# Chains first in the even mixer, and the odd mixer's running sums by transfers, its heads in pairs

## The chip, the cores and the metric

One of the eight cores of a Trainium2 chip runs the whole kernel. A core has TensorE (PE, with its weight loads shown apart as PEld), VectorE (DVE), ScalarE (ACT), GpSimd (POOL) and SyncE (SP), whose instruction streams run beside each other and meet at semaphores, and 16 DMA engines. The metric is the device time of one launch in microseconds. The kernel before takes 3082.39 us, the median of three runs (3081.61 to 3086.01).

## The reference

A decoder trunk of two layers over 288 tokens: 256 of a prompt and 8 x 4 new tokens of samples with 2048 tokens of past. Layer 0 mixes tokens by a gated MLP and a sparse attention (the "even mixer"), layer 1 by a Mamba-2 state space scan (the "odd mixer"); a gated MLP with a short convolution follows each.

```python
hp = hp + mp; hs = hs + ms                            # mixer of rmsnorm(h)
hp = hp + fp; hs = hs + fs                            # conv_ffn of rmsnorm(h)

# even mixer, samples: compressed attention, ranking, selected blocks
o_c, p_c = cmp_attend(q, k_cmp, v_cmp, pos)           # 2 x 64 blocks of cached pages
idx = select_blocks(p_c, pos, nb)                     # top 16 blocks of 64 tokens
o_s = sel_attend(q_rot, pos, idx, kb, vb)

# odd mixer: 64 heads in 8 groups, chunks of 128
acs = jnp.cumsum(dt * a, axis=-1)                     # running sums of each head
mix = cb[:, :, None] * jnp.exp(segsum(dt * a))        # exp(acs_i - acs_j), j <= i
y_diag = jnp.einsum('bgecij,bcjgep->bcigep', mix, xdt)
y_off = jnp.einsum(...) * jnp.exp(acs)
```

All is fp32. Products with weights are made from high and low parts: x_hi w_hi + x_lo w_hi + x_hi w_lo.

## The kernel before, in words

**The weight stream.** All weights pass once, as 6880 tiles of 128x128 ("slots"), each with three matmuls of 288 columns on PE ("mains": `xh,whi`, `xl,whi`, `xh,wlo`, or `hidh`/`hidl`), 20640 in all. A load `wraw<-in_w` on SP's queue brings 8 slots (512 KB, five buffers). Of each four slots ScalarE casts the high part (`whi`) and VectorE makes the low one (`wlo`). Results are summed in a PSUM tile `acc`, of which there are `PMAIN` = 2 beside five tiles `ps` for everything else. An evacuation multiplies by the reciprocal root mean square of the token (`rstd`) and writes it as `h`; it can run only once `make_rstd` (832) has made `rstd`: sums, a square root, a transposition `hl`, a spread over partitions by the matmul `ps<-rb,ones_r`, a copy.

**Phases.** The even mixer lasts from 0 to about 525 us, its MLP to 1370, the odd mixer to 2243, the second MLP to 3079.

**The order of the work.** It is planned when the program is built. Everything beside the stream is a generator, a "job"; `Trunk.step` (561) takes its next instruction and, when the planner's clock says that the inputs are ready and the engine free (within 0.02 us), writes it into the engine's stream, else it lets the job sleep. `tick` (600) steps the jobs in the order of their list between the mains. So each engine's order is fixed in the program, and an instruction whose input comes late holds up all behind it on its engine. `want` takes a buffer of a pool and `rel` gives it back.

**Even mixer.** `weigh` (1964) and `pool_blocks` (1990) read pages of the cache by gathers (`st<-in_ccmp,ptc`) and weigh them; `sample_cmp` (2032) attends to the compressed blocks, `rank` (2084) counts for each block how many beat it, and `sample` (2006) gathers the 16 chosen blocks and attends to them (`ps<-st,qzr` for scores, `po<-st,PT` for values).

**Odd mixer.** `dt_chain` (1093) makes the steps and, by matmuls with triangles, the running sums. They stay in SBUF as `csh`: 64 rows of high parts and 64 of low parts, a row for each head. The eight groups of heads come one after another: `ssd_old` (1290) reads and writes the samples' states (`po<-h,cms`, `xdd`), `ssd_new` (1304) adds to them (`ps<-xst,bst`), and `ssd_heads(g, q)` (1324) makes two heads: for each, a matmul with a column of `selc` spreads its running sums over 128 partitions (`ps<-csh,selc`), ScalarE makes L = relu(cs - csum), its exponentials, and `ec`; POOL multiplies `ec` with C; VectorE makes `mx` and, for the samples, `mxs`. Ten matmuls for each pair, a "burst" with weights 64 columns wide, then sum the outputs: `ps<-mx,xdt`, `ec,st`, `cmat,xdd`, `mxs,xds`.

In the profile all instructions carry the line of the helper that records them, L391 (L390 in the changed kernel), so they are told apart by tiles.

Of the kernel before, what the change touches and what calls it, by code (L numbers as in the profile page):

```python
# [10 lines left out]
F32 = mybir.dt.float32  # L11
F32R = mybir.dt.float32r
# [113 lines left out]
for _n, _w in (("tle", 128), ("tgt", 128), ("ble", 32), ("bgt", 32), ("selc", 64), ("srep", 32), ("srepT", 128),  # L126
               ("tmask", 256)):
    MATS[_n] = (sum(w for _, w in MATS.values()), _w)
# [387 lines left out]
class Job:  # L516
    def __init__(self, gen, at, room):
        self.gen, self.at, self.room, self.item, self.held = gen, at, room, None, []

class Trunk:
    def __init__(self, tc, I, O):
        self.clk = Clock()
        self.tc, self.I, self.O = tc, I, O
        self.nc, self.off = (Engines(tc.nc, self.clk, off) for off in (False, True))
        self.jobs, self.bg = [], []
        self.nbg, self.at, self.puts = 3, 0.0, 0
# [32 lines left out]
    def step(self, j):  # L561

        sent = None
        while True:
            self.cur = j
            if j.item is None:
                try:
                    j.item = j.gen.send(sent)
                except StopIteration:
                    for n in j.held:  # L570
                        Slots.back(n)
                    return False
# [24 lines left out]
            sent = it.pool.give(*it.a)  # L597
            j.held.append(sent.tensor.name)

    def tick(self):  # L600
        self.jobs = [j for j in self.jobs if j.at > self.now or self.step(j)]
        for j in list(self.bg)[:self.nbg]:
            if j.at <= self.now and not self.step(j):
                self.bg.remove(j)

    def wait(self, cond):

        for _ in range(200000):
            if cond():
                return  # L610
            self.at = max(self.now, min(j.at for j in self.jobs + self.bg[:self.nbg]))
            self.tick()
        raise RuntimeError([(j.gen.__name__, j.item) for j in self.jobs + self.bg])
# [46 lines left out]
    def run(self):  # L660
        tc, nc = self.tc, self.nc
        with ExitStack() as st:
            pool = lambda n, b, **k: Slots(st.enter_context(tc.tile_pool(name=n, bufs=b, **k)), b, self.clk)
            self.cst = pool("cst", 1)
            self.wraw = pool("wraw", 5)
            self.wsp = pool("wsp", AHEAD + 1)
            self.xp = pool("xp", 1)
            self.rms = pool("rms", 4)
            self.hsp = pool("hsp", 1, space=bass.MemoryType.DRAM).tile([128, KD, T], F32, name="hsp")
            self.pmain = pool("pmain", PMAIN, space=bass.MemoryType.PSUM)  # L670
            self.pold = pool("pold", 1, space=bass.MemoryType.PSUM)
            self.pside = pool("pside", 7 - PMAIN, space=bass.MemoryType.PSUM)
            st.enter_context(tc.manual_schedule())
            self.body()

    def body(self):
# [86 lines left out]
        self.wait(lambda: not self.jobs)  # L763
# [22 lines left out]
    def leave(self):  # L786
        if self.pst is not None:
            self.wait(lambda: not self.jobs)
            self.pst.close()
            self.pst = None  # L790
# [144 lines left out]
    def enter_f(self, l):  # L935
        nc = self.nc
        self.job(self.make_rstd())
# [80 lines left out]
    def enter_m1(self, l):  # L1018
        nc = self.nc
        self.job(self.make_rstd())  # L1020
# [4 lines left out]
        self.w4 = self.pool("w4", 4)  # L1025
# [10 lines left out]
        self.selc = t("selc", [128, 64], F32R)  # L1036
# [7 lines left out]
        self.csh = t("csh", [128, T], F32R)  # L1044
# [5 lines left out]
        self.mxs = deque(t(f"mxs{i}", [128, ST]) for i in range(4))  # L1050
# [18 lines left out]
    def odd_consts(self):  # L1069
# [4 lines left out]
        yield nc.vector.tensor_copy(self.selc, self.M("selc"))  # L1074
# [18 lines left out]
    def dt_chain(self, z):  # L1093
# [230 lines left out]
    def ssd_heads(self, g, q):  # L1324
# [3 lines left out]
        mx, ce, ms = [], [], []  # L1328
        for e in range(2):
            h = 8 * g + 2 * q + e  # L1330
            m = yield self.w4.want([128, PT], F32, name="mx")
            ec = yield self.w4.want([128, 128], F32, name="ec")
            L = yield wk.want([128, T], F32, name="L")
            pl = yield self.pside.want([128, T], F32, name="ps")
            yield self.mm(pl, self.selc[:, h:h + 1].to_broadcast([128, 128]), self.csh, start=True, stop=True)
            for lo, hi, r, c in ((0, 128, 128, 0), (128, 256, 128, 1), (256, 288, 32, 2)):
                yield nc.scalar.activation(L[:r, lo:hi], pl[:r, lo:hi], AF.Relu, bias=self.cs[:r, c, h:h + 1], scale=-1.0)
            yield nc.scalar.activation(ec, pl[:, 128:256], AF.Exp)
            self.rel(pl)
            yield nc.scalar.activation(L[:, :PT], L[:, :PT], AF.Exp, scale=-1.0)  # L1340
            yield nc.scalar.activation(L[:32, PT:], L[:32, PT:], AF.Exp, scale=-1.0)
            yield nc.gpsimd.tensor_tensor(ec, ec, C[:, 128:256], op=OP.mult)
            yield nc.vector.tensor_tensor(m[:, :PT], L[:, :PT], self.cbm[:, :PT], op=OP.mult)
            while not self.mxs:
                yield 0.3
            z = self.mxs.popleft()
            yield nc.vector.tensor_tensor(z[:32], L[:32, PT:], self.cbm[:32, PT:], op=OP.mult)
            ms.append(z)
            self.rel(L)
            mx.append(m)  # L1350
            ce.append(ec)
# [5 lines left out]
        ops = [self.mm(o[:, 0:128], self.xdt[:, 0, hc], mx[e][:, 0:128], start=True, stop=True) for e, o, hc in oh]  # L1357
        ops += [self.mm(o[:, 128:256], self.xdt[:, 1, hc], mx[e][:, 128:256], start=True, stop=False) for e, o, hc in oh]
        ops += [self.mm(o[:, 128:256], self.st[:, hc], ce[e], start=False, stop=True) for e, o, hc in oh]
        ops += [self.mm(o[:, 256:288], self.xdd[:, 0, hc], self.M("srep"), start=True, stop=False) for e, o, hc in oh]  # L1360
        ops += [self.mm(o[:, 256:288], self.xds[:, hc], ms[e], start=False, stop=True) for e, o, hc in oh]
        yield Burst(ops)
        self.mxs.extend(ms)
# [81 lines left out]
    def enter_m0(self, l):  # L1445
        nc, I = self.nc, self.I
        self.job(self.make_rstd())
# [65 lines left out]
        self.job(self.sample_cmp())  # L1513
        self.job(self.sample())
# [517 lines left out]
    def sample_cmp(self):  # L2032
# [14 lines left out]
        self.rel(kc)  # L2047
# [21 lines left out]
        self.rel(ps)  # L2069
        ps = yield self.pside.want([128, 2, 128], F32, name="ps")  # L2070
# [11 lines left out]
        self.job(self.rank())  # L2082

    def rank(self):
# [4 lines left out]
        a = yield self.w3.want([128, 512], F32, name="PT")  # L2089
        b = yield self.w3.want([128, 512], F32, name="PT")  # L2090
# [26 lines left out]
        yield nc.vector.tensor_scalar(self.selb.rearrange("p G n -> p (G n)"), ps, 14.5, NEG, op0=OP.is_gt, op1=OP.mult)  # L2117
        self.flags.add("rank")
# [152 lines left out]
```

## Time and profile before

| | |
|---|---|
| median of three runs | 3082.39 us (3081.61 to 3086.01) |
| the profiled execution | 3080.35 us |
| its span in the profile | 3078.6 us |
| PE busy | 3043.6 us (99%) |
| DVE, ACT, POOL busy | 70%, 52%, 24% |
| granted clock of TensorE, mean | 0.997 of full speed |
| HBM traffic | 189 GB/s over the span |

Matmuls overlap: a main takes about 295 ns from start to end, but one starts every 133 ns. A row of a timeline gives the start, the duration, the engine, the operation and, in brackets, how long the engine was idle before it and what released it. Waits of PE and of its weight loads (PEld) are listed apart: a weight load can wait while matmuls still run.

### The profile page before, as it was taken

To read this page: it belongs to the slowest core of one execution; us is meant where nothing else is said; L and a number is where in the kernel's file an instruction comes from. 1 tells how busy PE (TensorE), PEld (TensorE's weight loads), DVE (VectorE), ACT (ScalarE), POOL (GpSimd) and SP (SyncE) were. 2 spreads that over 40 slices of the span, in tenths; PEclk is the share of its full clock that TensorE was granted. 3 is DMA by queue.
4 is the path that set the end of the run, shared out by engine and by line. 5 is a ranking of instruction groups with operands and counts; after the bars stand their busy time and mean duration, and the time that the engine had idled before them with its cause. 6 is when DMAs were issued, how large, how long until landed. Compare 5 with 4: busy or idle time off the path is not lost.

```text
span 3078.6 us, 62211 instructions
## 1 busy us (share of the span) xinstructions
PE 3043.6 (99%) x23073; PEld 2943.9 (96%) x23073; DVE 2166.0 (70%) x4593; ACT 1614.4 (52%) x3229; POOL 724.6 (24%) x1029
## 2 busy tenths in 40 slices
PE   9999999999999999999999999999999999999999
PEld 8887889999999999999999999999999999999999
DVE  7876567775577557668888888885777647755764
ACT  6766545554455445555555555554455435544553
POOL 4535433100000000123445555530310000000000
PEclk8999999999999999999999999999999999999999
DMA  8987885444444444564555555554454444444454
GB/s 316 348 282 249 277 282 176 165 165 165 164 165 165 165 166 164 184 222 142 188 198 191 191 191 185 196 179 174 161 172 166 166 166 164 165 165 165 165 177 146
DMA packets 189760, 587.41 MB, mean 191 GB/s; under 512 B 23280, under 2 KB 43280, under 8 KB 189456
## 3 DMA queue, kind: packets, MB, share of 16 engines
q1 hardware_dynamic: 170256, 516.31, 48.7%
q0 software_dynamic: 19200, 67.12, 6.3%
q8 instruction: 182, 2.98, 0.4%
q14 instruction: 122, 1.00, 0.1%
HBM read 555.57 MB, written 27.78 MB: 189 GB/s over the span
## 4 chain that ended last, share of the span: by engine, by line
PE 89%; DVE 4%; POOL 3%; issue 1%; DMA 1%; ACT 1%; SPq 0%; DVEq 0%; ACTq 0%; POOLq 0%
PE acc L391 79%; PE ps L391 9%; DVE wlo L391 1%; PE po L391 1%; POOL ec L391 1%; DVE h L391 1%; DMA st<-in_ccmp,ptc 1%; POOL ssq L391 1%; POOL nrm L391 1%; DVE cv L391 1%; ACT whi L391 0%; DMA st<-in_cselv,ptv 0%; DVE mxs L391 0%; POOL st L391 0%; ACT L L391 0%
## 5 line engine op out<-in xcount | busy, mean ns | idle before, releaser
L391 DVE TENSOR_TENSOR wlo<-wraw,whi 128x512 fp32r<-128x512 f32 x1720 | 1230.4, 718 | 809.3 <-ACT whi L391 793.5
L391 ACT CAST whi<-wraw 128x512 fp32r<-128x512 f32 x1720 | 1058.5, 619 | 1187.6 <-PE acc L391 1062.0
L391 PE MATMUL acc<-xh,whi 128*128 128x288 f32 x5158 | 1552.9, 301 | 3.8 <-DVE h L391 3.4
L391 PE MATMUL acc<-xl,whi 128*128 128x288 f32 x5158 | 1524.4, 296 | 0.5 <-DVE xl L391 0.5
L391 PE MATMUL acc<-xh,wlo 128*128 128x288 f32 x5158 | 1519.8, 295 | 0.2 <-DVE wlo L391 0.2
L391 PEld LDWEIGHTS acc<-xh,whi 128*128 128x128 f32 x5158 | 969.7, 188 | 23.8 <-issue 15.1
L391 PEld LDWEIGHTS acc<-xl,whi 128*128 128x128 f32 x5158 | 971.4, 188 | 6.0 <-issue 3.8
L391 PEld LDWEIGHTS acc<-xh,wlo 128*128 128x128 f32 x5158 | 973.5, 189 | 0.7 <-DVE wlo L391 0.7
L391 PE MATMUL acc<-hidh,whi 128*128 128x288 f32 x1380 | 407.9, 296 | 0.0
L391 PE MATMUL acc<-hidl,whi 128*128 128x288 f32 x1380 | 407.1, 295 | 0.0
L391 PE MATMUL acc<-hidh,wlo 128*128 128x288 f32 x1380 | 406.1, 294 | 0.0
L391 POOL COPY fcv<-hx 128x18 f32<-128x18 f32 x176 | 37.3, 212 | 1399.4 <-DVE hx L391 1399.4
L391 PEld LDWEIGHTS acc<-hidh,wlo 128*128 128x128 f32 x1380 | 259.8, 188 | 0.0
L391 PEld LDWEIGHTS acc<-hidl,whi 128*128 128x128 f32 x1380 | 259.0, 188 | 0.0
L391 PEld LDWEIGHTS acc<-hidh,whi 128*128 128x128 f32 x1380 | 258.6, 187 | 0.0
L391 DVE SCALAR_TENSOR_TENSOR cv<-hx,prm,cv 128x304 f32<-128x304 f32 x352 | 185.9, 529 | 0.0
L391 POOL DMA_INDIRECT st<-in_ccmp,ptc x64 | 92.0, 1438 | 108.6 <-DVE S L391 22.3
L391 ACT ACTIVATE cv<-hx,prm 128x304 f32<-128x304 f32 x176 | 112.5, 641 | 0.8
L391 PE MATMUL ps<-xh,whi 128*128 128x288 f32 x314 | 94.6, 301 | 0.0
L391 PE MATMUL ps<-xh,wlo 128*128 128x288 f32 x314 | 93.1, 296 | 0.7 <-DVE wlo L391 0.7
L391 PE MATMUL ps<-xl,whi 128*128 128x288 f32 x314 | 93.1, 297 | 0.6 <-DVE xl L391 0.6
L391 DVE SCALAR_TENSOR_TENSOR cv<-cx,sw,cv 128x312 f32<-128x312 f32 x144 | 91.7, 641 | 2.6 <-ACT cv L391 2.6
(356 smaller groups left out, 2800.2 us busy)
## 6 DMA issues: line engine op xcount, KB each, us to landing
wraw<-in_w SPq DMA_DIRECT2D x859, 512.0 KB
h<-in_h SPq DMA_DIRECT2D x64, 256.0 KB
out_h<-h SPq DMA_DIRECT2D x64, 256.0 KB
st<-in_cselk SPq DMA_DIRECT2D x64, 128.0 KB
st<-in_cwk POOLq DMA_DIRECT2D x8, 512.0 KB
st<-in_cwv POOLq DMA_DIRECT2D x8, 512.0 KB
h<-in_xT SPq DMA_DIRECT2D x18, 144.0 KB
hsp<-h SPq DMA_DIRECT2D x4, 576.0 KB
```

The costliest lines, as they stand in the source:

```text
L391: self.f(*self.args, **self.kw)
```

## The change

Planner: a second list of jobs, chains, is stepped ahead of all others at each tick. `make_rstd` of every stage, `sample_cmp`, `sample` and `rank` become chains. An instruction of a chain that isn't PE's is written into its stream when its inputs are due within 0.3 us (0.02 for other jobs). `rank` starts in the middle of `sample_cmp` and takes over two of its tiles.

Odd mixer: the running sums are written once to DRAM (`csd`), and for each pair of heads a DMA on SP's queue reads two rows of them, repeated over 128 partitions, into `L` (128x2x288). `csh`, `selc` and their matmuls go. ScalarE works on `L` in place, the exponentials, `ec`, `mx` and `mxs` are made for both heads in one instruction. The planner waits for `L` and 1.2 us more before it places the first of these, and 2.5 us after the last input before it places the burst.

```diff
@@ class Job
-    def __init__(self, gen, at, room):
+    def __init__(self, gen, at, room, stand=0.02):
@@ class Trunk
+    def chain(self, gen):
+        self.chains.append(Job(gen, self.now, 4.0, 0.3))
...
-                elif t > max(self.now, free) + 0.02:
+                elif t > max(self.now, free) + (0.02 if it.eng == "tensor" else j.stand):
...
     def tick(self):
+        self.jobs, self.chains = self.chains + self.jobs, []
@@ enter_f, enter_m1, enter_m0
-        self.job(self.make_rstd())
+        self.chain(self.make_rstd())
@@ enter_m0
-        self.job(self.sample_cmp())
-        self.job(self.sample())
+        self.chain(self.sample_cmp())
+        self.chain(self.sample())
@@ dt_chain
-        yield nc.scalar.copy(self.csh[:64], p2)
-        yield nc.vector.tensor_tensor(self.csh[64:128], p2, self.csh[:64].bitcast(F32), op=OP.subtract)
+        csh = yield wk.want([64, T], F32, name="dz")
+        yield nc.scalar.copy(csh, p2)
         self.rel(p2)
+        yield nc.sync.dma_start(self.csd, csh)
@@ ssd_heads
-        mx, ce, ms = [], [], []
-        for e in range(2):
-            h = 8 * g + 2 * q + e
-            m = yield self.w4.want([128, PT], F32, name="mx")
-            ec = yield self.w4.want([128, 128], F32, name="ec")
-            L = yield wk.want([128, T], F32, name="L")
-            pl = yield self.pside.want([128, T], F32, name="ps")
-            yield self.mm(pl, self.selc[:, h:h + 1].to_broadcast([128, 128]), self.csh, start=True, stop=True)
...
+        h0 = 8 * g + 2 * q
+        L = yield wk.want([128, 2, T], F32, name="L")
+        yield nc.sync.dma_start(L, self.csd[None, h0:h0 + 2, :].to_broadcast([128, 2, T]))
+        mx = yield wk.want([128, 2, PT], F32, name="mx")
+        ce = yield wk.want([128, 2, 128], F32, name="ec")
+        yield [L]
+        yield 1.2
+        yield nc.scalar.activation(ce, L[:, :, 128:256], AF.Exp)
+        for e in range(2):
             for lo, hi, r, c in ((0, 128, 128, 0), (128, 256, 128, 1), (256, 288, 32, 2)):
...
+        yield nc.vector.tensor_tensor(mx, L[:, :, :PT], self.cbm[:, None, :PT].to_broadcast([128, 2, PT]), op=OP.mult)
...
+        yield [mx, ms, ce]
+        yield 2.5
         yield Burst(ops)
@@ sample_cmp
-        self.rel(kc)
+        self.keep(kc)
...
+        two = yield self.w3.want([128, 512], F32, name="PT")
+        self.keep(two)
+        self.chain(self.rank(kc, two))
...
         self.rel(t, po, st)
-        self.job(self.rank())
```

VectorE in the head of the even mixer, before. `rms`, `hl`, `rt`, `rb` are `make_rstd`'s; `PT`, `S` and `y` belong to the weighing of cache pages; `wlo` is the stream's and `h` the first evacuation.

```order
L391 TENSOR_TENSOR hl<-rms,hl 96x3
L391 SCALAR_TENSOR_TENSOR S<-st,wpq 128x256 x2
L391 TENSOR_TENSOR wlo<-wraw,whi 128x512
L391 COPY rt<-ps 6x96
L391 SCALAR_TENSOR_TENSOR S<-st,wpq 128x256 x2
L391 TENSOR_TENSOR wlo<-wraw,whi 128x512
L391 TENSOR_TENSOR rb_93<-rt,prm 6x288
L391 SCALAR_TENSOR_TENSOR S<-st,wpq 128x256 x2
L391 TENSOR_TENSOR wlo<-wraw,whi 128x512
L391 SCALAR_TENSOR_TENSOR y<-st,wpq 128x256 x2
L391 TENSOR_TENSOR wlo<-wraw,whi 128x512
L391 TENSOR_TENSOR h<-acc,rstd 128x288 x2
```

The same place after:

```order
L390 TENSOR_TENSOR hl<-rms,hl 96x3
L390 TENSOR_TENSOR PT<-wp,st_159 128x128
L390 TENSOR_TENSOR wlo<-wraw,whi 128x512
L390 TENSOR_REDUCE wpq<-PT 128x4
L390 TENSOR_SCALAR qs<-prm 128x1
L390 TENSOR_TENSOR wsb<-wsb,emat 32x256
L390 COPY rt<-ps 6x96
L390 TENSOR_TENSOR rb_96<-rt,prm 6x288
L390 TENSOR_TENSOR wlo<-wraw,whi 128x512 x2
L390 TENSOR_TENSOR h<-acc,rstd 128x288 x2
L390 TENSOR_TENSOR h<-ps,rstd 128x288
L390 SCALAR_TENSOR_TENSOR S<-st,wpq 128x256 x4
```

The chain from `hl` to `h` now stands ahead of all the `S` and `y` products of gathered pages. On PE `ps<-rb,ones_r` moves from main 237 to main 192.

PE in a group of the odd mixer, before, from the end of the samples' old states (`po`):

```order
L391 MATMUL po<-h_20125,cms 32x512
L391 MATMUL po<-h_20134,cms 32x512
L391 MATMUL ps<-csh,selc 128x288
L391 MATMUL acc<-xh,whi 128x288
L391 MATMUL acc<-xl,whi 128x288
L391 MATMUL acc<-xh,wlo 128x288
L391 MATMUL acc<-xh,whi 128x288
L391 MATMUL acc<-xl,whi 128x288
L391 MATMUL acc<-xh,wlo 128x288
L391 MATMUL ps<-xst,bst 128x512
L391 MATMUL ps<-csh,selc 128x288
```

The same place after:

```order
L390 MATMUL po<-h_20001,cms 32x512
L390 MATMUL po<-h_20031,cms 32x512
L390 MATMUL acc<-xh,whi 128x288
L390 MATMUL acc<-xl,whi 128x288
L390 MATMUL acc<-xh,wlo 128x288
L390 MATMUL acc<-xh,whi 128x288
L390 MATMUL acc<-xl,whi 128x288
L390 MATMUL acc<-xh,wlo 128x288
L390 MATMUL ps<-xst,bst 128x512
```

The selector matmuls are gone, the rest stands as before. What feeds ScalarE instead is on SP's queue, after:

```order
L390 DMA wraw<-in_w 128x1024
L390 DMA h_20887<-in_h 128x512
L390 DMA h_20939<-in_h 128x512
L390 DMA h_20960<-in_h 128x512
L390 DMA L<-csd 128x576
L390 DMA out_h<-h_19930 128x512
L390 DMA out_h<-h_19988 128x512
L390 DMA wraw<-in_w 128x1024
```

The read of `L` for a pair stands between a weight load with three loads of sample states (`h<-in_h`) and the stores of the states of the group before (`out_h<-h`).

## Rows read from the trace of the kernel before

**Rows 1.** The page, part 1: busy us, share, instructions of each engine.

```profile
PE 3043.6 (99%) x23073; PEld 2943.9 (96%) x23073; DVE 2166.0 (70%) x4593; ACT 1614.4 (52%) x3229; POOL 724.6 (24%) x1029
```

**Rows 2.** Chain of waits, whole execution: start, us, what the chain ran through.

```profile
21.96 3.55 DMA wraw<-in_w
...
36.73 8.55 DMA st<-in_ccmp,ptc
...
536.16 746.97 PE acc L391 x5604
```

**Rows 3.** Windows, even mixer: us, busy PE/PEld/DVE/ACT/POOL, clock, DMA share, GB/s.

```profile
40.00:47.60 7.60, 4.16 (x32) 3.96 (x31) 5.88 (x14) 5.63 (x13) 6.09 (x4) 1.00 1.04 402
47.60:61.40 13.80, 13.80 (x65) 11.86 (x66) 7.22 (x24) 5.79 (x15) 4.09 (x5) 0.51 0.82 272
61.40:150.00 88.60, 88.60 (x670) 78.29 (x670) 77.85 (x208) 64.11 (x148) 52.14 (x36) 0.98 0.91 337
260.00:452.00 192.00, 188.15 (x1493) 158.11 (x1491) 116.62 (x374) 104.53 (x244) 90.60 (x87) 1.00 0.82 274
```

**Rows 4.** Timeline of PE at the first evacuation.

```profile
43.43 0.30 PE L391 MATMUL ps<-rb,ones_r 128*128 128x288 f32 x1
...
47.56 0.46 PE L391 MATMUL acc<-xh,whi 128*128 128x288 f32 x1 [3.44 <-DVE h L391]
```

**Rows 5.** Timeline of ACT at the same place.

```profile
45.31 0.51 ACT L391 ACTIVATE st<-st,wpq 128x256 f32<-128x256 f32 x1 [0.74 <-DMA st<-in_ccmp,ptc]
45.72 0.60 ACT L391 CAST whi<-wraw 128x512 fp32r<-128x512 f32 x1
```

**Rows 6.** Groups of PE: busy us, mean ns, idle before and its releasers.

```profile
L391 PE MATMUL ps<-csh,selc 128*128 128x288 f32 x64 | 19.2, 320 | 2.4 <-DVE xdd L391 1.9 <-DVE h L391 0.5
```

**Rows 7.** Waits of PE, 1430 to 2060 us: total us, times, longest.

```profile
PE ps L391 <- DVE mxs L391: 5.1, 7, 0.7
PE ps L391 <- DVE h L391: 3.9, 8, 0.5
PE ps L391 <- DVE xdd L391: 1.9, 7, 0.3
```

**Rows 8.** Waits of PE's weight loads, same stretch.

```profile
PEld ps L391 <- DVE h L391: 9.3, 15, 0.8
...
PEld ps L391 <- DVE mxs L391: 6.2, 9, 0.8
...
PEld ps L391 <- DVE cv L391: 5.9, 7, 0.8
PEld ps L391 <- DVE xdd L391: 5.1, 8, 0.8
```

**Rows 9.** Timeline of PE: a double burst, and one that stalls.

```profile
1481.46 0.29 PE L391 MATMUL acc<-xh,wlo 128*128 128x288 f32 x1
1481.68 0.66 PE L391 MATMUL ps<-mx,xdt 128*64 128x128 f32 x8
...
1482.59 0.64 PE L391 MATMUL ps<-mx,xdt 128*64 128x128 f32 x8
...
1483.82 0.29 PE L391 MATMUL acc<-xl,whi 128*128 128x288 f32 x1
...
1630.32 0.28 PE L391 MATMUL ps<-mxs,xds 128*64 128x32 f32 x2
1631.32 0.30 PE L391 MATMUL ps<-mxs,xds 128*64 128x32 f32 x2 [0.72 <-DVE mxs L391]
```

**Rows 10.** One group of the odd mixer: its window, then groups of ACT and PE.

```profile
1553.20:1634.30 81.10, 79.52 (x627) 74.64 (x626) 70.80 (x143) 46.32 (x113) 41.55 (x45) 1.00 0.55 188
...
L391 ACT CAST whi<-wraw 128x512 fp32r<-128x512 f32 x40 | 24.0, 615 | 16.8 <-PE acc L391 14.8 <-issue 1.1 <-ACT th L391 0.6
...
L391 PE MATMUL po<-h,cms 128*32 128x512 f32 x16 | 1.9, 598 | 0.0
```

**Rows 11.** Waits of PE, 0 to 470 us.

```profile
PE po L391 <- DMA st<-in_cselv,ptv: 1.7, 2, 1.4
```

More of the change, by code (lines that the diff above doesn't have):

```diff
@@ L125 @@
 MATS = {}
-for _n, _w in (("tle", 128), ("tgt", 128), ("ble", 32), ("bgt", 32), ("selc", 64), ("srep", 32), ("srepT", 128),
+for _n, _w in (("tle", 128), ("tgt", 128), ("ble", 32), ("bgt", 32), ("srep", 32), ("srepT", 128),
                ("tmask", 256)):
@@ L139, in const_mats @@
         ble=same & (t[:, None] <= t), bgt=same & (t[:, None] > t),
-        selc=i[:, None] % 64 == np.arange(64),
         srep=i[:, None] % 32 == t, srepT=t[:, None] == i % 32,
@@ L516 @@
 class Job:
-    def __init__(self, gen, at, room):
+    def __init__(self, gen, at, room, stand=0.02):
         self.gen, self.at, self.room, self.item, self.held = gen, at, room, None, []
+        self.stand = stand
 class Trunk:
@@ L526, in __init__ @@
         self.nc, self.off = (Engines(tc.nc, self.clk, off) for off in (False, True))
-        self.jobs, self.bg = [], []
+        self.jobs, self.chains, self.bg = [], [], []
         self.nbg, self.at, self.puts = 3, 0.0, 0
@@ L610, in wait @@
                 return
-            self.at = max(self.now, min(j.at for j in self.jobs + self.bg[:self.nbg]))
+            self.at = max(self.now, min(j.at for j in self.chains + self.jobs + self.bg[:self.nbg]))
             self.tick()
@@ L669, in run @@
             self.hsp = pool("hsp", 1, space=bass.MemoryType.DRAM).tile([128, KD, T], F32, name="hsp")
+            self.csd = pool("csd", 1, space=bass.MemoryType.DRAM).tile([64, T], F32, name="csd")
             self.pmain = pool("pmain", PMAIN, space=bass.MemoryType.PSUM)
@@ L762, in body @@
             self.evac(pending.popleft()[0])
-        self.wait(lambda: not self.jobs)
+        self.wait(lambda: not self.jobs and not self.chains)
         self.wait(lambda: not self.bg)
@@ L787, in leave @@
         if self.pst is not None:
-            self.wait(lambda: not self.jobs)
+            self.wait(lambda: not self.jobs and not self.chains)
             self.pst.close()
@@ L1019, in enter_m1 @@
         nc = self.nc
-        self.job(self.make_rstd())
+        self.chain(self.make_rstd())
         self.nbg = 3
@@ L1024, in enter_m1 @@
         self.w3 = self.pool("w3", 3)
-        self.w4 = self.pool("w4", 4)
         self.w8 = self.pool("w8", NB)
@@ L1035, in enter_m1 @@
         self.sw = t("sw", [128, 48, 5])
-        self.selc = t("selc", [128, 64], F32R)
         self.dtt = t("dtt", [128, 3, 64])
@@ L1043, in enter_m1 @@
         self.ets = t("ets", [128, NB, 64])
-        self.csh = t("csh", [128, T], F32R)
         self.xdt = t("xdt", [128, 2, 512])
@@ L1049, in enter_m1 @@
         nc.gpsimd.memset(self.xds[64:128], 0.0)
-        self.mxs = deque(t(f"mxs{i}", [128, ST]) for i in range(4))
+        self.mxs = deque(t(f"mxs{i}", [128, 2, ST]) for i in range(2))
         for z in self.mxs:
@@ L1073, in odd_consts @@
         yield nc.vector.tensor_scalar(self.sw[:, :, 4], self.P("sb", 0, 48), 0.5, None, op0=OP.mult)
-        yield nc.vector.tensor_copy(self.selc, self.M("selc"))
+        pass
         self.flags.add("consts")
@@ L1327, in ssd_heads @@
         C = self.C[g]
-        mx, ce, ms = [], [], []
-        for e in range(2):
-            h = 8 * g + 2 * q + e
-            m = yield self.w4.want([128, PT], F32, name="mx")
-            ec = yield self.w4.want([128, 128], F32, name="ec")
-            L = yield wk.want([128, T], F32, name="L")
-            pl = yield self.pside.want([128, T], F32, name="ps")
-            yield self.mm(pl, self.selc[:, h:h + 1].to_broadcast([128, 128]), self.csh, start=True, stop=True)
-            for lo, hi, r, c in ((0, 128, 128, 0), (128, 256, 128, 1), (256, 288, 32, 2)):
[L1337 to L1351, printed above, removed]
@@ new lines, in ssd_heads @@
+        yield nc.scalar.activation(L[:, :, :PT], L[:, :, :PT], AF.Exp, scale=-1.0)
+        yield nc.scalar.activation(L[:32, :, PT:], L[:32, :, PT:], AF.Exp, scale=-1.0)
+        yield nc.gpsimd.tensor_tensor(ce, ce, C[:, None, 128:256].to_broadcast([128, 2, 128]), op=OP.mult)
+        yield nc.vector.tensor_tensor(mx, L[:, :, :PT], self.cbm[:, None, :PT].to_broadcast([128, 2, PT]), op=OP.mult)
+        while not self.mxs:
+            yield 0.3
+        ms = self.mxs.popleft()
+        yield nc.vector.tensor_tensor(ms[:32], L[:32, :, PT:], self.cbm[:32, None, PT:].to_broadcast([32, 2, ST]), op=OP.mult)
@@ L1352, in ssd_heads @@
+        self.rel(L)
         while "old" not in self.sdone:
@@ L1356, in ssd_heads @@
         oh = [(e, py[64 * e:64 * e + 64], slice(128 * q + 64 * e, 128 * q + 64 * e + 64)) for e in range(2)]
-        ops = [self.mm(o[:, 0:128], self.xdt[:, 0, hc], mx[e][:, 0:128], start=True, stop=True) for e, o, hc in oh]
-        ops += [self.mm(o[:, 128:256], self.xdt[:, 1, hc], mx[e][:, 128:256], start=True, stop=False) for e, o, hc in oh]
-        ops += [self.mm(o[:, 128:256], self.st[:, hc], ce[e], start=False, stop=True) for e, o, hc in oh]
+        ops = [self.mm(o[:, 0:128], self.xdt[:, 0, hc], mx[:, e, 0:128], start=True, stop=True) for e, o, hc in oh]
+        ops += [self.mm(o[:, 128:256], self.xdt[:, 1, hc], mx[:, e, 128:256], start=True, stop=False) for e, o, hc in oh]
+        ops += [self.mm(o[:, 128:256], self.st[:, hc], ce[:, e], start=False, stop=True) for e, o, hc in oh]
         ops += [self.mm(o[:, 256:288], self.xdd[:, 0, hc], self.M("srep"), start=True, stop=False) for e, o, hc in oh]
-        ops += [self.mm(o[:, 256:288], self.xds[:, hc], ms[e], start=False, stop=True) for e, o, hc in oh]
+        ops += [self.mm(o[:, 256:288], self.xds[:, hc], ms[:, e], start=False, stop=True) for e, o, hc in oh]
+        yield [mx, ms, ce]
+        yield 2.5
         yield Burst(ops)
-        self.mxs.extend(ms)
+        self.mxs.append(ms)
         k = 4 * g + q
@@ L1446, in enter_m0 @@
         nc, I = self.nc, self.I
-        self.job(self.make_rstd())
+        self.chain(self.make_rstd())
         one = self.pool("one", 1)
@@ L2117, in rank @@
         yield nc.vector.tensor_scalar(self.selb.rearrange("p G n -> p (G n)"), ps, 14.5, NEG, op0=OP.is_gt, op1=OP.mult)
+        self.cur.held += [a.tensor.name, b.tensor.name]
         self.flags.add("rank")
```

6 lines of the change are left out of this document (3 added, 3 removed).

## The prediction

> **What bounds the kernel now.** First the page's busy times: PE 3043.6 of 3078.6 us, 99%, while VectorE has 70 and ScalarE 52 [rows 1]. So only what PE does, and what PE waits for, can change the time; work saved on ScalarE or VectorE is worth nothing by itself. Then the chain of waits: its long pieces are matmul runs such as 5604 in 746.97 us [rows 2], which is 0.1333 us for one "main" (a 288-column matmul of the weight stream). In the even mixer the chain also holds transfers: 8.55 us from issue to landing for a gather of cache pages, 3.55 us for a 512 KB weight load [rows 2]. Third the windows: in the first 150 us the DMA engines are busy at a share of 0.82 to 1.04, and right after a stall at 44 us PE's granted clock is 0.51 of full speed, 1.2 instead of 2.4 GHz, for 13.8 us [rows 3]. Last the waits of PE and of its weight loads in the eight groups of the odd mixer [rows 7, 8]. The gated MLP stages are full of mains and the change leaves them as they are.
>
> **Odd mixer, work that goes.** 64 selector matmuls (`ps<-csh,selc`) leave PE [rows 6]; nothing replaces them there. Each is 128x288 like a main and follows at a main's pitch: 64 x 0.133 = **-8.5 us**. Their own 295 to 320 ns is latency under which the next one starts. The ScalarE and VectorE instructions that leave (98 and 66 by the order of the two kernels) lie on engines with room: ScalarE's weight casts wait 14.8 us per group for PE to give buffers free [rows 10]. They count only through waits.
>
> **Odd mixer, waits.** PE rows: it stood 5.1 us for mxs, 3.9 for the evacuation h, 1.9 for xdd, together 10.9 [rows 7]. Weight-load rows: h 9.3, mxs 6.2, cv 5.9, xdd 5.1, together 26.5 [rows 8]. A weight load that waits is hidden as long as a matmul runs, so 10.9 is the lower bound and 26.5 the upper. One stalled burst tells where between: its mxs matmuls start at 1630.32 and 1631.32 [rows 9], 1.00 us apart where 0.1 is usual, so 0.9 are lost where the row writes 0.72. All four waits have one root: several small instructions per head queued on VectorE ahead of what PE wants. After the change the mask products mx and mxs are half as many, the burst is planned 2.5 us after its last input, and the selector matmuls that waited for xdd, cv and h no longer exist. I take the middle, **-19**.
>
> One rule speaks against so much. The Trainium skill, "TensorE: Matmul & The Clock Gate", section "Step-by-step: what each phase is for", says that PE's queue pulls weight loads ahead of matmuls in flight; by it alone the waits of the weight loads cost nothing, only 10.9 go, and the sum would be 8 us higher (an estimate). The 0.9 lost at 1631 is more than the idle time in its row, so the trace follows the rule only in part.
>
> **Odd mixer, what is added.** Per group the eight heads' bursts stood in three runs before, one of them a double one; after, by the order, in four lone bursts. A double one takes 1483.82 - 1481.46 = 2.36 us [rows 9] with two burst bodies of 0.91 (1481.68 to 1482.59) and two mains' pitches in it: 2.36 - 1.82 - 0.27 = 0.27 us to turn PE from 128x128 to 128x64 weights and back. One more per group: 8 x 0.27 = **+2.2**.
>
> New is the transfer of L: 295 KB broadcast from DRAM for each pair, 32 of them, on SP's queue, behind weight loads and stores. No row shows one. From its issue to ScalarE's first read the order of the changed kernel has, with the po run at 1.9 us [rows 10], a burst with its turn at 1.2 and 0.24 (512 columns against 288) for an xst matmul: pair 1, 15 mains, po and two xst, 4.4 us; pair 2, 21 mains, most of po and two xst, 5.0; pair 3, 26 mains and a burst, 4.7; pair 4, 19 mains, 2.5. From below L lands like the 512 KB load, 3.55 us: only pair 4 is late, by 1.0, and the planned 2.5 us before the burst cover it: 0. From above like the gather, 8.55 us [rows 2]: late by 4.2, 3.6, 3.8, 6.0, less 2.5 each = 7.6 us per group, 61 in all. In these groups the DMA share is 0.55 [rows 10], and the gather's 8.55 fell where it was 0.91 and more, so the value lies near the lower end: **+4**, half a microsecond per group for pair 4.
>
> The Trainium skill, "DMA: Bandwidth & Descriptors", section "Anatomy of one DMA — SWDGE (gpsimd) path", gives about 2.0 us fixed plus bytes over 436 GB/s, for L an estimate of 2.7 us; by it this term is 0 and the sum 4 us lower. No row shows such a transfer.
>
> **Even mixer, head.** PE's row at 43.43 is the matmul that spreads the reciprocal root mean square (rb) over partitions; then three mains and a stop of 3.44 us for the first evacuation h [rows 4]. PE had used up its accumulators. Between rb and h ScalarE had a weighing that waited 0.74 us for a gather, at 45.31, and the weight cast only at 45.72 [rows 5], whose wlo VectorE has to make before it gets to h. The clock then fell to 1.2 GHz for 13.8 us [rows 3], in which PE did half as much: 6.9 us lost. After the change rb is at main 192 in place of 237 by the order, 45 x 0.133 = 6.0 us earlier, more than the 3.44 of the stop, and the evacuations follow at once on VectorE. PE's accumulators hold to main 240, 6.4 us behind rb. So the stop goes, and with it the fall: -3.4 - 6.9 = **-10.3**. What is late next? A PE that is 10 us earlier meets gathers and weight loads that are not: from 61 to 150 us DMA is at 0.91 [rows 3], so about 0.09 x 88.6 + 0.18 x 13.8 = 10.5 us are free, just the gain. Given back 0 to 10.3; I take **+3**, because the free share holds nearly all of it.
>
> **Even mixer, second half.** The ranking of the sample's blocks starts earlier, and the 16 runs of `st,qzr` and `st,PT` that read selected K/V blocks stand at mains 1314 to 1884 instead of 1266 to 2070 by the order: 234 mains, 31.2 us less room. Before, 260 to 452 us moved 192 x 274 GB/s = 52.6 MB [rows 3]. The stretch after has 161 us and 78 fewer 64 KB weight tiles, 5.1 MB: 47.5 MB, 295 GB/s. At 274 GB/s it would take 173 us, 12 more than it has; at the 337 of the head [rows 3], 141, none. PE's waits for such a landing were 1.7 us before [rows 11]. Between 0 and 12 I take **+4**: the rate that it needs is nearer to 274 than to 337, and the share would be 0.88. The other chains (make_rstd in the later stages) stand where they stood within a few mains: 0.
>
> **Sum.** -8.5 - 19 + 2.2 + 4 - 10.3 + 3 + 4 = -24.6. The profiled execution took 3080.35 us (span 3078.6), the median of the runs 3082.39, 2.0 more: 3080.35 - 24.6 + 2.0 = **3058 us**. A measurement of this kernel can tell 0.2%, 6 us, from no change.
>
> **Rivals.**
> - Only the matmuls go. Bursts wait as long for pairs as they did for heads, and the gathers eat the head's gain: -8.5 + 2.2 = -6.3, **3076**. For it: PE stands in line behind VectorE, at 70.80 of 81.1 us in a group [rows 10], and one late input is soon replaced by the next. Against it: the mask products are halved in number and the burst gets a margin.
> - Everything goes: all 26.5, the whole head, no late landing: -8.5 - 26.5 + 2.2 - 10.3 = -43.1, **3039**. For it: the stalled burst lost more than its row shows. Against it: the weight-load rows overlap with matmuls in flight, and DMA is at 0.82 to 0.91 in the even mixer.
> - Slower, by L. It queues on SP behind stores of states and a 512 KB load, and its rows come as 128 copies; if that lands as late as the gather, 8.55 us, the 61 us replace the 4: 3058 - 4 + 61 = **3115**. It decides from about 7.5 us after issue: there 0.6 + 0.3 + 2.5 = 3.4 us per group, 27 in all, eat the other 28.6. For it: nothing else in a group depends on a landing so shortly after its issue. Against it: DMA share 0.55, no gather near.
> - That the change doesn't do what it says is excluded: the order has 64 selector matmuls less and rb 45 mains earlier.
>
> **How the numbers follow.** Forecast 0.64, with its own range 3045 to 3070 (waits 10.9 to 26.5, head given back 0 to 10.3, second half 0 to 12, not all at one end). Only the matmuls 0.18, half of it within 6 us of before. Everything 0.09. Slower 0.09, a tenth of it within 6 us. Faster: 0.64 + 0.09 + 0.09 = 0.82; same 0.09 + 0.01 = 0.10; slower 0.08. The range 3039 to 3081 leaves out half of "everything" and nearly all of "slower", about 0.15.
>
> **What would show it.** In the page after: no `csh,selc` group, PE about 25 us less. At 35 to 62 us: no stop of 3 us before h, and the granted clock at 1.0; if the stop stays, the -10.3 fails. In the odd groups: the waits for mxs, h, xdd and cv together under 8 us on PE's rows, the period of a group near 78 instead of 81; a row "ACT ec from DMA L" of several us with PE waiting for mx or ec is the slower rival. From 260 to 420 us: DMA share near 0.88, and waits for st under 5 us. The prediction is wrong as a whole if a group's period stays above 80.

## The result: 3105 us, slower by 0.8%

The changed kernel takes 3105.22 us in the median of five runs (3100.67 to 3113.62), the kernel before 3082.39: a ratio of 1.0079 with a 95% interval of 1.0066 to 1.0091. Forecast were 3058 us, the range ended at 3081. The profiled execution took 3100.67 us, its span is 3098.9.

PE is busy 7 us less than before [rows 1], and the span is 20 us longer. Part 1 of the page after:

```profile
PE 3036.6 (98%) x23009; PEld 2938.8 (95%) x23009; DVE 2193.4 (71%) x4527; ACT 1610.3 (52%) x3131; POOL 700.4 (23%) x995
```

Since both kernels run the same 20640 mains in the same order, the clearest comparison is the start of the n-th main in both traces. Main 8800, before the odd mixer, starts at 1343.2 instead of 1350.7 us; main 13600, after its last group, at 2152.8 instead of 2133.0. So the stages ahead of the odd mixer gained 7.5 us and the odd mixer lost **27.4**. I call this difference (main 8800 to 13600, against 782.3 us before) the odd mixer's loss.

PE's waits there (total, times, longest), after; before they were 5.1 for mxs, 3.9 for h, 1.9 for xdd [rows 7]:

```profile
PE ps L390 <- DVE mx L390: 23.1, 23, 1.2
PE ps L390 <- POOL ssq L390: 17.3, 7, 2.6
```

The second is new. After a group's fourth burst VectorE evacuates the output (`h<-h,prm,ps`), GpSimd multiplies, squares and sums it (ssq), and PE sums ssq over partitions. Here is PE at one such place, start and duration in front: the fourth burst, the sums, and the mains after them.

```profile
1660.82 0.29 PE L390 MATMUL ps<-mxs,xds 128*64 128x32 f32 x4
1668.46 0.67 PE L390 MATMUL ps<-ones,ssq 128*96 128x1 f32 x6 [2.36 <-POOL ssq L390]
...
1670.27 0.43 PE L390 MATMUL acc<-xh,whi 128*128 128x288 f32 x1
1670.50 0.44 PE L390 MATMUL acc<-xl,whi 128*128 128x288 f32 x1
```

From 1670.3 us the mains follow at 0.24 us instead of 0.133: after five of the seven stops the granted clock fell to 1.2 GHz, 20.4 us in all, and at half the pace these cost another 10.2. VectorE at the same place:

```profile
1662.32 0.67 DVE L390 TENSOR_TENSOR wlo<-wraw,whi 128x512 fp32r<-128x512 f32 x1
1663.09 0.53 DVE L390 SCALAR_TENSOR_TENSOR h<-th,cv 128x256 f32<-128x256 f32 x2
1663.54 1.12 DVE L390 SCALAR_TENSOR_TENSOR cv<-cx,sw,cv 128x312 f32<-128x312 f32 x2
1664.57 0.51 DVE L390 SCALAR_TENSOR_TENSOR h<-h,prm,ps 128x288 f32<-128x288 f32 x1
```

The evacuation starts 3.7 us behind the burst, after casts and instructions of the next convolution that stand ahead of it on VectorE. In the kernel before, the burst's last matmuls stood at 1657.78 and the evacuation 0.62 us behind:

```profile
1658.40 0.50 DVE L391 SCALAR_TENSOR_TENSOR h<-h,prm,ps 128x288 f32<-128x288 f32 x1
```

VectorE was nearly full in this part of a group in both kernels, from the states' matmuls to the sums. The windows (us; busy PE, PEld, DVE, ACT, POOL; clock; DMA share; GB/s) of before, then of after:

```profile
1614.00:1662.00 48.00, 46.32 (x381) 42.69 (x381) 45.57 (x88) 28.10 (x81) 38.05 (x40) 1.00 0.64 215
```

```profile
1617.30:1668.30 51.00, 45.76 (x380) 42.45 (x378) 50.66 (x85) 28.38 (x70) 35.89 (x36) 1.00 0.67 226
```

45.57 of 48 us before, 50.66 of 51 after, with 85 instructions in place of 88. The pairs are not what fills it: sixteen `mx` and `mxs` of 7.78 us in sum became eight of 6.70. In their place stand five more instructions of the stream and the convolution, and some instructions are longer beside GpSimd: `mx` takes 0.68 us where GpSimd rests (1651.4 to 1654.7) and 1.30 where it was already at work. VectorE after, then GpSimd:

```profile
1651.30 0.68 DVE L390 TENSOR_TENSOR mx<-L,cbm 128x512 f32<-128x512 f32 x1
...
1658.42 1.30 DVE L390 TENSOR_TENSOR mx<-L,cbm 128x512 f32<-128x512 f32 x1
```

```profile
1654.72 0.61 POOL L390 COPY sco<-cx 128x27 f32<-128x27 f32 x1 [3.28 <-DVE cx L390]
...
1658.24 0.93 POOL L390 TENSOR_TENSOR ssq<-ssq,nrm 128x288 f32<-128x288 f32 x1
1659.11 0.68 POOL L390 COPY cx<-scv 128x24 f32<-128x24 f32 x1
```

In the even mixer the stop before the first evacuation fell from 3.44 [rows 4] to 1.31 us and half clock from 13.8 to 3.4 us; DMA then runs at 0.96 instead of 0.91 [rows 3], and the stretch of the K/V blocks at 0.88:

```profile
45.50:48.90 3.40, 3.40 (x16) 1.46 (x14) 2.54 (x11) 1.64 (x6) 1.88 (x2) 0.50 1.03 417
61.40:150.00 88.60, 88.43 (x681) 78.97 (x681) 79.67 (x208) 66.48 (x156) 45.61 (x35) 1.00 0.96 351
260.00:420.00 160.00, 156.89 (x1272) 130.17 (x1269) 94.60 (x332) 91.97 (x226) 87.28 (x86) 1.00 0.88 297
```

### The profile page after: what moved, and what is told of

It is laid out like the page before. It is cut to its first block, busy times and chain, and to the rows that moved or that the text cites. A ratio compares the mean times of both kernels' runs of the same rounds, so it can differ in the third digit from the quotient of the medians.

```text
span 3098.9 us, 61893 instructions
## 1 busy us (share of the span) xinstructions
PE 3036.6 (98%) x23009; PEld 2938.8 (95%) x23009; DVE 2193.4 (71%) x4527; ACT 1610.3 (52%) x3131; POOL 700.4 (23%) x995
## 4 chain that ended last, share of the span: by engine, by line
PE 86%; DVE 4%; DMA 4%; issue 2%; ACT 1%; POOL 1%; SPq 1%; DVEq 0%; ACTq 0%; POOLq 0%
PE acc L390 77%; PE ps L390 8%; PE po L390 1%; DMA st<-in_ccmp,ptc 1%; DVE cv L390 1%; DVE wlo L390 1%; DMA out_h<-h 1%; DMA L<-csd 1%; DVE h L390 1%; POOL ssq L390 0%; DVE mx L390 0%; ACT whi L390 0%; DMA st<-in_cselk 0%; DVE y L390 0%; POOL nrm L390 0%
## 5 line engine op out<-in xcount | busy, mean ns | idle before, releaser
L390 PE MATMUL acc<-xh,whi 128*128 128x288 f32 x5198 | 1570.2, 302 | 3.2 <-DVE h L390 1.3
L390 PEld LDWEIGHTS acc<-xh,whi 128*128 128x128 f32 x5198 | 979.9, 189 | 33.5 <-issue 23.7
L390 PEld LDWEIGHTS acc<-xl,whi 128*128 128x128 f32 x5198 | 981.7, 189 | 7.5 <-issue 3.8
L390 PEld LDWEIGHTS acc<-xh,wlo 128*128 128x128 f32 x5198 | 983.8, 189 | 1.1 <-DVE wlo L390 1.1
L390 DVE SCALAR_TENSOR_TENSOR cv<-cx,sw,cv 128x312 f32<-128x312 f32 x144 | 101.1, 702 | 0.2
L390 DVE TENSOR_TENSOR hx<-acc,rstd 128x256 f32<-128x256 f32 x350 | 90.0, 299 | 0.2
L390 POOL TENSOR_TENSOR h<-h,ets 128x512 f32<-128x512 f32 x64 | 88.5, 1402 | 0.0
L390 PE MATMUL ps<-xh,wlo 128*128 128x288 f32 x274 | 80.9, 295 | 0.7 <-DVE wlo L390 0.7
```

Source lines behind the costliest of these rows:

```text
L390: self.f(*self.args, **self.kw)
```

## The experiments

Ratios are to the kernel before on the same chip. "Odd" is the odd mixer's loss in the profiled execution, as defined above (27.4 for the change). The theories: **M**, PE reaches the sums before VectorE and GpSimd, and a planned margin decides who pays; **L**, L lands late; **V** or **B**, VectorE's amount of work sets the pace; **P** or **G**, GpSimd stretches VectorE's work; **O**, the place of one instruction; **A**, any new order meets a late engine.

**The two halves.** `even_only` has the chains and the odd mixer of before, `odd_only` the reverse.

> Only the planner's chains (even mixer, make_rstd), the odd mixer as before. Both theories of the odd mixer leave this alone: by the traces main 9200 comes 6.9 to 7.5 us earlier in the changed kernel, so about 3075 us, 7 below before. If the even half also costs (a rival of its own), it would be at or above 3082.

> Only the odd mixer's transfers, pairs and delays; the even mixer as before. If the two halves are independent: before plus the 28 us that the odd mixer lost in the trace, about 3110 us. If the odd half is only slow because the even half shifted the program: near 3082.

Measured: `even_only` 0.9976 (0.9965 to 0.9987), odd +0.8; `odd_only` 1.0099 (1.0082 to 1.0116), odd 28.7. The halves are independent (the two ratios multiplied give 1.0075), and the odd one is the whole loss.

**The margins.** `no_delay` takes the planned 2.5 us ahead of the bursts away, `norm_delay` adds one ahead of the sums.

```diff
 # no_delay, in ssd_heads
-        yield [mx, ms, ce]
-        yield 2.5
         yield Burst(ops)
 # norm_delay, in ssd_norm
         while len(self.sdone) < 5:
             yield 0.4
+        yield [self.ssq]
+        yield 2.5
```

> The changed kernel without the planned 2.5 us ahead of each burst. Theory M (the planned margin lets VectorE fall behind PE without PE noticing, and the lag is paid at the sums of squares after the fourth burst: 17.3 us of waits and 20.4 us at half clock): the waits come back to the bursts, the sums wait under 4 us in all, clock 1.0, and the time falls by 10 to 20 us, to 3085 to 3095. Theory L (L lands late, 5.2 us in the median after issue): bursts stand earlier and L as late, so the waits grow, 3105 to 3125.

> The changed kernel with a planned 2.5 us ahead of the sums of squares too. Theory M: the sums' wait (17.3 us) and the clock's fall (about 10 us lost) go, 3078 to 3084. Theory B (VectorE is the bound of the stretch, the wait only moves on to the next matmul that needs it): 3100 to 3110. Theory L: the late L still delays ScalarE (16.2 us) but PE is not held at the sums; at most half of the gain, 3090 to 3100.

Measured: `no_delay` 1.0095 (1.0079 to 1.0112), odd 33.0: the waits moved to the bursts as M said, but half clock rose to 34.1 us instead of going, and the time, 3110.73 us, is not M's but lies in L's range; `norm_delay` 1.0009 (0.9999 to 1.0019), odd 5.0, M's figure nearly, and better than L or B allowed. PE's waits, first without the delay, then with the margin:

```profile
PE ps L390 <- DVE mx L390: 37.7, 15, 3.4
PE ps L390 <- POOL ssq L390: 3.7, 6, 0.6
```

```profile
PE ps L390 <- DVE mx L390: 11.6, 14, 1.2
PE acc L390 <- DVE cx L390: 5.3, 3, 2.3
PE ps L390 <- DVE hl L390: 4.5, 1, 4.5
PE ps L390 <- POOL ssq L390: 2.3, 5, 0.8
```

41.4 us against 40.4: without the delay the same lag is paid at the bursts. With a margin at both places most of it is paid nowhere. That VectorE catches up in the second half of a group is how I read it: there it is busy 22.65 of 32.2 us in the changed kernel.

**GpSimd, and the landing of L.** `no_ets` leaves out GpSimd's decay of the states, `l_wait4` plans 4.0 in place of 1.2 us behind L.

```diff
 # no_ets, in ssd_new
-            yield nc.gpsimd.tensor_tensor(self.h8(t), self.h8(t), self.hb(self.ets[:, b, hs]), op=OP.mult)
 # l_wait4, in ssd_heads
-        yield 1.2
+        yield 4.0
```

> The changed kernel without GpSimd's 64 products of the samples' old states with their decay (h<-h,ets, 11.3 us per group; this leaves the decay out of the states). Theory P (VectorE's instructions with both operands in SBUF stretch while GpSimd works, 109.6 us of stretch between 1430 and 2080 us against 86.1 before, and that is what makes VectorE late): the stretch falls below 70 us, PE's waits for mx from 23.1 to under 8 and for ssq from 17.3 to under 6, 3070 to 3085 us. Rival (VectorE's own queue of work, not GpSimd, sets the lag): waits stay above 30 in sum, 3098 to 3110.

> The changed kernel with 4.0 in place of 1.2 us between L's planned landing and its first planned read. Theory L: ScalarE's waits for L (16.2 us in 9 places) go under 3 us, its casts come in time, and the time falls by 10 us or more, to 3085 to 3095. Theory M (the margin hides VectorE's lag, the sums pay): the waits for L go too, but PE's waits for mx and ssq stay at 35 to 45 us, 3098 to 3112.

The stretch in the first is the sum of what VectorE's instructions take above the tenth percentile of their form. Counted so between 1430 and 2080 us it is about 87 us before, 118 after and 65 in `no_ets`; 86.1 and 109.6 in the expectation are not what this count gives. Measured: `no_ets` 1.0039 (1.0028 to 1.0050), odd 20.5; no wait for mx left, but the sums waited longer. `l_wait4` 1.0047 (1.0033 to 1.0062), odd 23.9, slower than L's range; ScalarE no longer waits for `ec`'s L, and PE's waits for mx fall from 23.1 to 3.8, which M had not forecast. PE's waits of `no_ets`, then of `l_wait4`:

```profile
PE ps L390 <- POOL ssq L390: 21.2, 7, 3.6
```

```profile
PE ps L390 <- POOL ssq L390: 18.8, 7, 2.8
PE acc L390 <- ACT L L390: 4.6, 3, 1.8
PE ps L390 <- DVE hl L390: 4.5, 1, 4.5
PE ps L390 <- DVE mx L390: 3.8, 7, 1.3
```

So each of the two takes the bursts' waits away, and neither takes away the sums'. Their cause is not the same, though. In `no_ets` VectorE stood idle before each of the seven late evacuations (14.5 us in all): it waited for ScalarE, ScalarE for a copy of GpSimd (24.0 us in seven waits), and this copy stood behind a long instruction of GpSimd, in five of the seven cases a product of 3.35 us. The product had started 0.16 us behind an `mx`, which kept its 0.68 us. VectorE, GpSimd, ScalarE and VectorE again:

```profile
1659.68 0.68 DVE L390 TENSOR_TENSOR mx<-L,cbm 128x512 f32<-128x512 f32 x1
1659.84 3.35 POOL L390 TENSOR_TENSOR h<-h,zt 128x288 f32<-128x288 f32 x1 [1.95 <-DVE h L390]
1665.86 0.65 ACT L390 ACTIVATE cv<-cx,sw 128x312 f32<-128x312 f32 x1 [3.53 <-POOL cx L390]
1666.54 1.12 DVE L390 SCALAR_TENSOR_TENSOR cv<-cx,sw,cv 128x312 f32<-128x312 f32 x2 [2.28 <-ACT cv L390]
```

In the changed kernel VectorE has no such wait; there it is late with work of its own. So `no_ets` doesn't clear GpSimd: with 64 products less, it was itself what came late.

**More margin.** Both with 2.5 us ahead of the sums.

```diff
 # norm_chain, in ssd
-        self.back(self.ssd_norm(g))
+        self.chain(self.ssd_norm(g))
 # norm_chain_d4, also in ssd_heads
-        yield 2.5
+        yield 4.0
```

> The changed kernel with 2.5 us planned ahead of the sums of squares, as before, and with the normalisation after them as a chain. In the last group the run without the chain lost 4.7 us to VectorE's hl behind casts, and 3.4 us of half clock: with the chain both go, 3085.6 - 6 to 8 = 3078 to 3080. If that stall only moves on: 3084 to 3087.

> The same with 4.0 in place of 2.5 us ahead of the bursts. Theory M: the waits for mx that are left (11.6 us) go, and nothing else takes their place as the sums have a margin of their own: 3068 to 3074. Theory B (VectorE bounds the stretch, each wait only moves on): 3078 to 3086.

Measured: `norm_chain` 0.9991 (0.9978 to 1.0005), odd 4.3; `norm_chain_d4` 0.9977 (0.9965 to 0.9988), odd 4.7. The waits for hl went in the first and those for mx doubled (22.6 us); in the second mx fell to 2.4 and `acc` waited 15.5 for cx: as B said, the wait moved on.

**The evacuation's place, and the delay by itself.** On a chip where the kernel before took 3126.46 us. `tail_chain` puts what follows the burst into a chain; `before_delay` is the kernel before with the 2.5 us alone; `best_a` is `tail_chain` with `norm_chain`'s two edits, `best_b` also with 4.0 us ahead of the bursts. The new generator `ssd_tail` holds the evacuation, the product and the squares.

```diff
 # tail_chain, in ssd_heads
+        self.keep(py)
+        self.chain(self.ssd_tail(g, q, py))
...
 # before_delay, in ssd_heads of the kernel before
+        yield [*mx, *ms, *ce]
+        yield 2.5
         yield Burst(ops)
```

> The changed kernel with what follows a burst (evacuation on VectorE, product, squares and their sum on GpSimd) as a chain, so that the evacuation stands right behind the burst on VectorE, 30 mains ahead of the sums as in the kernel before. Theory O (it is only the place of that evacuation, 3.7 to 4.0 us behind the fourth burst instead of 0.6, that costs): evacuation within 1 us, the sums' wait from 17.3 to under 3 us, no half clock, 3078 to 3085. Theory M (VectorE is 2 us late by then, wherever it stands, since the planned 2.5 us kept PE from waiting): evacuation 2 to 3 us behind the burst, sums wait 1.3 to 2 us in a group, 9 to 14 in all, 3088 to 3098.

> The kernel before with one thing of the change: 2.5 us planned ahead of each burst. Theory M: the waits for mxs (5.1 us) go, VectorE falls further behind, and the sums of squares wait 1 to 3 us in a group: 3085 to 3100. If only the transfers or the pairs cost: 3077 to 3084.

> The changed kernel with the tail behind a burst and the normalisation as chains and 2.5 us planned ahead of the sums. Theory M: no wait for ssq, the waits for mx as with the chain alone (11 to 23 us): 3072 to 3080. Theory B (VectorE bounds the stretch): 3080 to 3086.

> The same with 4.0 us planned ahead of the bursts. Theory M: the waits for mx under 3 us and no other of size: 3064 to 3072. Theory B: VectorE is late for the next evacuation of a convolution instead (acc waiting for cx, 15 us where 4.0 was tried), 3074 to 3082.

Measured: `tail_chain` 1.0122 (1.0097 to 1.0147), odd 42.9: the evacuation still came 3.1 to 3.9 us behind the burst, so O falls. M had the sign right and the size wrong: the sums waited 23.1 us, not 9 to 14. `before_delay` 1.0091 (1.0060 to 1.0121), odd 24.8: the delay alone costs the kernel before about as much as the whole change does, more than M's figure. There most of the waiting is not at the sums but one step on, in the normalisation:

```profile
PE ps L391 <- DVE hl L391: 11.7, 6, 6.2
PE ps L391 <- DVE rb L391: 6.0, 7, 0.9
PE ps L391 <- POOL ssq L391: 4.4, 2, 2.7
```

`best_a` 1.0045 (1.0032 to 1.0059), odd 25.1, slower than either theory had it; `best_b` 0.9975 (0.9961 to 0.9989), odd 6.7, as B said, with `acc` waiting 11.5 us for cx. That `best_a` loses 25.1 us with a margin ahead of the sums, where `norm_chain` loses 4.3, is not explained.

**Less work on VectorE; pairs and transfers apart.** `no_hadd` and `before_no_hadd` leave 64 additions out of VectorE; `pairs_csh` is the kernel before with pairs but selector matmuls, `heads_dma` with the transfers but single heads, both without the delay ahead of the bursts.

```diff
 # no_hadd, before_no_hadd, in ssd_new
-            yield nc.vector.tensor_tensor(t, t, pu, op=OP.add)
 # pairs_csh, in ssd_heads: pl by self.mm(pl, self.selc[...], self.csh) for each head as before
+        yield nc.vector.tensor_tensor(mx, L[:, :, :PT], self.cbm[:, None, :PT].to_broadcast([128, 2, PT]), op=OP.mult)
 # heads_dma, in ssd_heads: L by the transfer, then for each head
+            yield nc.vector.tensor_tensor(m, L[:, e, :PT], self.cbm[:, :PT], op=OP.mult)
```

> The changed kernel without VectorE's 64 additions of new to old states (h<-h,ps, 8 of 0.67 us in a group; this leaves the new samples' contribution out of the states). Theory V (from po to the sums of squares VectorE is full, 50.7 of 51.0 us, and sets the pace there, so work taken from PE gives nothing and lag is paid wherever PE has no margin): 5 us per group of room, the waits for mx and ssq (40 us) and the half clock go, ratio to before 0.992 to 0.999. Rival G (it is GpSimd that holds VectorE up): as without the decays on GpSimd, 1.002 to 1.006, with the wait for ssq left.

> The kernel before without the same 64 additions. Theory V: VectorE was nearly full there too (45.6 of 48.0 us), so the waits on PE's rows (11) and of its weight loads (26) go: ratio 0.993 to 0.997. If PE sets the pace of the kernel before in this half of a group: 0.998 to 1.001.

> The kernel before with the heads in pairs, but with the selector matmuls and without a planned delay (z buffers 11 instead of 12). If the two-head instructions on VectorE cost by themselves: 1.006 to 1.010, as the change. Theory V (VectorE's time counts; 2 x 0.51 us become 1.26, less two mxs): 1.000 to 1.005.

> The kernel before with the transfers in place of the selector matmuls, but heads one by one and without a planned delay. If the transfers cost by themselves: 1.006 to 1.010. Theory V: 64 matmuls less on PE give nothing and VectorE's work is as before, 0.998 to 1.004; were PE the bound, 8.5 us less, 0.997.

Measured: `no_hadd` 1.0015 (1.0005 to 1.0024), odd 10.8; `before_no_hadd` 1.0034 (1.0022 to 1.0047), odd 13.7; `pairs_csh` 1.0175 (1.0157 to 1.0194), odd 53.1; `heads_dma` 1.0105 (1.0085 to 1.0125), odd 27.9. V falls as it was stated: with 5 us less to do in each group VectorE is still late at the sums, and the kernel before even gets slower. Its work does count, as the loss fell from 27.4 to 10.8 us and the waits for mx from 23.1 to 1.4. The wait for ssq that G expected is left, and G's 1.002 to 1.006 touches the interval, so GpSimd is not excluded here either. PE's waits of `no_hadd`, `before_no_hadd`, `pairs_csh`, `heads_dma`:

```profile
PE ps L390 <- POOL ssq L390: 21.0, 7, 3.3
```

```profile
PE ps L391 <- POOL ssq L391: 10.0, 7, 1.4
```

```profile
PE ps L391 <- POOL ssq L391: 21.9, 7, 3.1
```

```profile
PE ps L390 <- DVE mx L390: 27.3, 11, 4.0
```

Pairs alone and transfers alone each cost as much as the change or more, and more than either expectation had. All eleven kernels with a new order of the odd mixer and no margin ahead of the sums lost 10.8 to 53.1 us there, whatever was added or left out.

**A version with all margins.** `l4_norm_chain` joins `l_wait4` and `norm_chain`, `l4_norm4_chain` has 4.0 us ahead of the sums.

> The changed kernel with 4.0 us after L's landing, 2.5 us planned ahead of the sums of squares, and the normalisation as a chain. Theory M (what costs is that PE reaches the sums before VectorE and GpSimd; a planned margin at each place where PE meets them hides their lag): the run with 4.0 us for L had only 3.8 us of waits for mx left beside 18.8 at the sums and 5 in the last group; with both gone the odd mixer is 8 to 12 us shorter than before and the even one 4 to 7: ratio 0.993 to 0.996. Theory A (any new order of the odd mixer meets a late engine somewhere): 0.997 to 1.001.

> The same with 4.0 us ahead of the sums. Theory M: the evacuation comes 3.3 to 4.1 us behind the fourth burst and the sums need 7.5 us; 48 mains are 6.4, 60 are 8.0, so here no wait at the sums at all where 2.5 us leaves up to 1: 0 to 6 us better than the other, 0.992 to 0.996. Theory A: 0.997 to 1.001.

Measured: `l4_norm_chain` 0.9979 (0.9968 to 0.9989), odd **-5.0**; `l4_norm4_chain` 0.9981 (0.9972 to 0.9991), odd -2.9. The odd mixer now gains, as M said, but not the 8 to 12 us of its figure, and both ratios lie in A's range, 0.997 to 1.001. PE's waits of the first:

```profile
PE acc L390 <- ACT L L390: 6.4, 4, 1.8
PE ps L390 <- POOL ssq L390: 4.2, 7, 0.7
PE ps L390 <- DVE mx L390: 3.6, 8, 1.1
```

It is 0.2% faster than the kernel before, and so is `even_only`; the intervals don't tell the two apart. So the new odd mixer, with all its margins, is not shown to make the whole kernel faster than the old one does.

## Why the prediction was wrong

- **Work that goes, -8.5, and the extra turn, +2.2:** right in what goes and comes: the 64 selector matmuls are gone from the trace, and 32 lone bursts stand where there were 24 runs of bursts. Their price was not measured by itself.
- **Waits of the odd mixer, -19: the step that failed.** It said that the waits for mxs, h, xdd and cv have one root, small instructions on VectorE, and that halving them takes the waits away. These waits did go (1.0 us of them is left, in the weight loads' rows), but waits for mx and for the sums came in their place: 40.4 us instead of 10.9, and half clock cost 10.2 more. With the -6.3 us of work that makes 33.4, where 27.4 were lost; the 6 us between are open. I had judged VectorE by 70.80 of 81.1 us in a group [rows 10]; in the half in which PE depends on it, it was at 95%. The sums stood 36 mains or 4.8 us behind the burst, where the chain from the burst over the evacuation to ssq needed 7.6 to 7.9. `norm_delay` brings back 22.4 of the 27.4 us by a margin there, so the meeting of PE with the late chain is the cause of most of the loss. That the 2.5 us ahead of the burst made VectorE late is not the whole of it: `before_delay` loses 24.8 us by this delay alone, but `no_delay` without it loses 33.0.
- **Late L, +4, and the rival "slower, by L", 3115:** near in time (3105) by luck. L landed 5.2 us after issue in the median, at most 6.5, between the bounds of 3.55 and 8.55 and short of the 7.5 from which that rival was to decide. The 2.7 us that the prediction also cites belongs to transfers issued by GpSimd; L goes out on SP's queue, and the measured time decides. The rival's sign did show, ScalarE waiting for L and PE for mx:

```profile
ACT ec L390 <- DMA L<-csd: 16.2, 9, 3.1
```

  But planned 2.8 us later these waits vanish, and the odd mixer's loss falls by 3.5 us only (27.4 to 23.9).
- **Head of the even mixer, -10.3 + 3, and its second half, +4:** main 400 came 6.2 us earlier, main 800 6.9, so the head kept 6.9 of the 7.3 forecast. This is in part luck: the stop and the fall of the clock gave about 7.3 us (2.1 and 5.2) instead of 10.3, and hardly any of it was lost again. The K/V blocks' stretch ran at 297 GB/s and a share of 0.88, as worked out, but PE waited for landings only 1.4 us, and between mains 800 and 2400 it gained 0.7 us instead of losing 4. So the stages ahead of the odd mixer gained 7.5 us in this execution, where the sum had 3.3. The gain varies: in the eleven profiled executions of these chains outside the slower chip main 8800 starts 12.7 us earlier to 1.6 later than in that of before, 3.9 earlier in the mean.
- **The test "a group's period near 78, over 80 means wrong":** 85.2 us (1615.4 to 1700.5), as the prediction named for its own failure. PE's busy time fell by 7.0 us, not by about 25.

Not settled: why the orders differ so much in VectorE's lag, and how much of it is GpSimd's doing. The planner books 0.60 us for a two-head `mx` whatever GpSimd does, and the trace shows 0.68 to 1.53; that its clock runs ahead of VectorE for this reason was not tried by itself, for instance with a cost that knows of GpSimd.

## What to carry to other kernels

A share of busy time is to be read in the stretch in which the bounding engine depends on the other one: here 87% over a group hid 95% in the 48 us that matter. A planned margin ahead of one wait need not remove a lag; in `before_delay` and `norm_chain_d4` the wait came back at the next place without one. Look for that place before you add it, and measure the chain that ends there. In a program whose order is fixed ahead, even work left out can cost time, so an edit's worth is that of the order it makes.

## What the runs showed of the hardware

VectorE and GpSimd hold each other up. `mx`, with both operands in SBUF, took 0.67 to 0.69 us alone or nearly so, and up to 1.53 us where GpSimd was already at work (changed kernel); `h<-h,ps`, which reads PSUM, took 0.67 us each of its 64 times. The other way, GpSimd's product `h<-h,zt` took 0.81 us at the evacuation in the kernel before and 3.35 us where `mx` had started 0.16 us ahead of it (`no_ets`). A stop of PE of 2.4 to 2.6 us at the sums was followed by 3.4 us or more at 1.2 GHz in five of seven cases of the changed kernel.
